# Seven block products for half of the gated-conv tiles, masked exponents and chunks from both ends in the SSD of a hybrid encoder

## Chip, cores, metric

The kernel runs on one core of one Trainium2 chip. The metric is device time in microseconds (us) of one execution; three runs are taken and their median counts. TensorE (PE) multiplies, VectorE (DVE), ScalarE (ACT) and GpSimd (POOL) work elementwise, SyncE (SP) issues the DMA transfers. Each engine takes its instructions in the order in which the built program lists them and waits on semaphores for the others.

## What is computed

A batch of one sequence of 1,024 tokens with 1,024 features goes through two layers, all in fp32. The change lies in the first, which multiplies the input by one weight matrix, feeds two head groups, and multiplies their outputs by a second matrix:

```python
z, xbc, dt_raw, sc_bg, sc_cg, sc_h, sc_gate = _split(x @ w_in, EVEN_SIZES)
xs, bm, cm = _split(silu(depthwise_conv(xbc, conv_w, (2, 1)) + conv_b), (SSD_INNER, 512, 512))
# A: SSD in both directions, chunks of 128 tokens, 4 groups of 4 heads, dt = softplus(dt_raw + bias)
cs = cumsum(dt * a)                               # within a chunk
L  = exp(where(l >= s, cs[l] - cs[s], -inf))      # decay inside a chunk, per head
y_diag = einsum(C B^T * L, x * dt)
state  = state * exp(cs[-1]) + einsum(B, exp(cs[-1] - cs), x * dt)
y_off  = einsum(C, state, exp(cs))
y_a = rms_norm((y_fwd + y_bwd) * silu(z), norm_g)
# B: short gated convolution
y_b = sc_bg * depthwise_conv(sc_cg * sc_h, sc_conv_w, (1, 1)) * silu(sc_gate)
out = layer_norm(alpha * x + concat(y_a, y_b) @ w_out)
```

## The kernel before

Every fp32 product is made of three fp32r products: an operand is cast to fp32r (`hi`, on ScalarE) and the rest is subtracted (`lo`, on VectorE, `split`), and hi·hi, hi·lo and lo·hi are summed in PSUM. A weight tile is 1,024 x 128; applied to all tokens it takes eight steps (`op_fm`, one per 128 input rows), each of six matmuls of 512 columns (`mm6`): 48 matmuls, shown as `gps`. The first layer has 48 such tiles: 16 for x, B and C of the SSD (each followed by a convolution of four taps on VectorE, `cacc`, and a SiLU, `xfm`), and 32 for the gated convolution, called `br` (four projections for each of eight blocks of 128 channels; the tile results are `bru`, `bra`, `brt`). z is computed token block by token block (`zps`).

`main_plan` writes the order of the work by hand. The SSD runs over four head groups. A group has a second phase (`op_p2`, `op_p2s`; the first is the projection) in which each of the eight chunks is transposed (`xps`) and its state is computed (`sps`) and added to the forward scan; `op_p2b` then runs the backward scan, six serial steps of a decay on GpSimd and an addition on VectorE (`hin`). In the third phase `op_p3f` builds a chunk's decay matrix times C·B^T: two broadcasts from DRAM (`E`, `tb`), Relu in eight pieces of 128 columns, `Dm` in four, a maximum, an Exp of 512 columns, two products, and the split into `Mh`, `Ml`. `op_p3x` splits the state and x. `op_p3b` multiplies: `yo` from the state, `yd` from `Mh` and `Ml`, one block of eight `yd` matmuls a chunk; the sums `to` and `ta` follow on VectorE and GpSimd.

Between these, `pull(n)` takes n steps of projection tiles from a queue: 6 ahead of the second phase (`FB`), 4 ahead of the third (`FC`), 7 after each chunk of the third (`F3`). They fill TensorE while the other engines prepare the next chunk. x of the next group goes to the front of the queue at the third phase, B and C behind it. The tile framework's scheduler then may move instructions of one engine ahead of others that wait.

Weight tiles come by DMA into two rotating buffers (`wraw`) and are split one tile ahead. At the start x arrives in eight pieces through four buffers of its own (`xraw`), is split, and feeds the small product for dt (`dtg`). At the end, the normalised SSD output is read back, scaled, transposed (`yat`) and split beside the last `br` tiles (`op_ya`, half a row block at a time), and `outproj0` multiplies (`ops`).

## Time and profile before

| | us |
|---|---|
| median of three runs (1444.60 to 1447.18) | 1445.21 |
| the profiled execution | 1445.73 |
| its span, first to last instruction | 1444.0 |
| TensorE busy | 1416.2 |
| VectorE busy | 921.9 |
| ScalarE busy | 749.1 |
| GpSimd busy | 480.5 |

The profile was taken in one execution. Busy times of TensorE overlap between neighbouring matmuls, so its rate is read from how many start in a stretch. The SSD lies between about 65 us (first `zps`) and 705 us (last `yd`); the tail of the gated tiles ends at 728 us and the output product of the first layer follows.

### The profile page before, as it was taken

The page shows a single profiled execution, that of the slowest core. Times are in us where ns is not written, and L with a number is a line of the kernel's source. Part 1 is how long each engine was busy: PE and PEld are TensorE (multiplying, and loading weights), DVE is VectorE, ACT ScalarE, POOL GpSimd, SP SyncE. Part 2 cuts the span into 40 slices and gives each one's busy share as a digit, 9 for nine tenths or more (in the row PEclk, how much of TensorE's full clock was granted, in tenths as well). Part 3 has the DMA queues.
Part 4 walks back from the last instruction along what each step waited for, and adds up shares of the span by engine and source line. Part 5 has one row for each costly group of instructions (what it writes and reads, how often), then busy time and mean ns, then how long its engine had stood idle before and what let it go on. Part 6 is the DMA issues. An engine that isn't in the chain of part 4 may idle for free.

```text
span 1444.0 us, 20351 instructions
## 1 busy us (share of the span) xinstructions
PE 1416.2 (98%) x7454; PEld 1208.9 (84%) x7454; DVE 921.9 (64%) x1608; ACT 749.1 (52%) x1567; POOL 480.5 (33%) x479
## 2 busy tenths in 40 slices
PE   7999999999999999999989999999999999999997
PEld 5898888888898888988868888898888888988886
DVE  5837666666687665647683543733326888888485
ACT  5447654576447773566443332522224788888510
...
DMA packets 46483, 118.57 MB, mean 82 GB/s; under 512 B 5808, under 2 KB 10288, under 8 KB 46384
## 3 DMA queue, kind: packets, MB, share of 16 engines
...
## 4 chain that ended last, share of the span: by engine, by line
PE 44%; DVE 4%; issue 1%; ACT 1%; DMA 0%; POOL 0%; DVEq 0%; ACTq 0%; POOLq 0%
PE ops L377 4%; PE ops L378 4%; PE ops L380 4%; PE tps L1211 3%; PE fps L371 3%; PE fps L372 3%; PE fps L370 3%; PE o1ps L377 2%; PE o1ps L380 2%; PE o1ps L378 2%; PE yps L1226 2%; PE sps L370 2%; PE sps L372 2%; PE sps L371 2%; PE yps L1225 2%
## 5 line engine op out<-in xcount | busy, mean ns | idle before, releaser
L377 PE MATMUL gps<-xhi,whi 128*128 128x512 f32 x768 | 302.2, 394 | 0.0
L378 PE MATMUL gps<-xlo,whi 128*128 128x512 f32 x768 | 301.7, 393 | 0.0
L380 PE MATMUL gps<-xhi,wlo 128*128 128x512 f32 x768 | 242.6, 393 | 0.0
L249 DVE TENSOR_TENSOR wlo<-wraw,whi 128x1024 fp32r<-128x1024 f32 x100 | 137.5, 1377 | 109.4 <-ACT whi L248 99.5
L248 ACT CAST whi<-wraw 128x1024 fp32r<-128x1024 f32 x100 | 104.7, 1049 | 131.4 <-DMA wraw<-in_wt_dram 41.3
L377 PEld LDWEIGHTS gps<-xhi,whi 128*128 128x128 f32 x768 | 144.4, 188 | 29.0
L378 PEld LDWEIGHTS gps<-xlo,whi 128*128 128x128 f32 x768 | 144.4, 188 | 29.0
L380 PEld LDWEIGHTS gps<-xhi,wlo 128*128 128x128 f32 x768 | 142.9, 188 | 28.7
L1197 POOL TENSOR_SCALAR pt<-pt,sm 128x1024 f32<-128x1024 f32 x64 | 72.9, 1140 | 114.2 <-DVE sm L1196 63.3
L467 POOL TENSOR_TENSOR xdl<-xd,xdh 128x512 fp32r<-128x512 f32 (+1 forms) x32 | 36.9, 1153 | 206.5 <-ACT xdh L466 166.0
L467 DVE TENSOR_TENSOR PT<-tps,PT 128x512 fp32r<-128x512 f32 x128 | 84.1, 681 | 12.6 <-ACT PT L466 12.4
L1191 DVE TENSOR_REDUCE nm<-sps 128x1 f32<-128x1024 f32 x64 | 77.9, 1217 | 9.5 <-PE sps L372 9.2
L467 POOL TENSOR_TENSOR hl<-hin,hh 128x512 fp32r<-128x512 f32 (+1 forms) x32 | 38.7, 1210 | 135.4 <-ACT hh L466 135.4
L814 POOL TENSOR_TENSOR rs<-rs,neghalf 128x1 f32<-128x1 f32 x16 | 12.9, 808 | 209.4 <-DMA wraw<-in_wt_dram 81.4
L1195 ACT ACTIVATE pt<-sps,nm 128x1024 f32<-128x1024 f32 x64 | 71.8, 1122 | 17.4 <-DVE nm L1192 13.1
L466 ACT CAST PT<-tps 128x512 fp32r<-128x512 f32 x128 | 69.9, 588 | 16.2 <-PE tps L1211 15.6
L370 PE MATMUL fps<-x1hi,whi 128*128 128x512 f32 x192 | 74.9, 390 | 0.0
L372 PE MATMUL fps<-x1hi,wlo 128*128 128x512 f32 x192 | 74.8, 389 | 0.0
L371 PE MATMUL fps<-x1lo,whi 128*128 128x512 f32 x192 | 74.7, 389 | 0.0
L370 PE MATMUL zps<-whi,xhi 128*128 128x256 f32 x256 | 73.9, 289 | 0.0
L372 PE MATMUL zps<-whi,xlo 128*128 128x256 f32 x256 | 72.4, 283 | 0.0
L371 PE MATMUL zps<-wlo,xhi 128*128 128x256 f32 x256 | 72.3, 282 | 0.0
...
## 6 DMA issues: line engine op xcount, KB each, us to landing
wraw<-in_wt_dram SPq DMA_DIRECT2D x100, 512.0 KB, 3.6
...
```

The source lines that it names most:

```text
L248: nc.scalar.copy(out=hi, in_=raw)
L249: nc.vector.tensor_tensor(out=lo, in0=raw, in1=hi.bitcast(F32), op=ALU.subtract)
L370: nc.tensor.matmul(out, shi, mhi, start=start, stop=False)
L371: nc.tensor.matmul(out, shi, mlo, start=False, stop=False)
L372: nc.tensor.matmul(out, slo, mhi, start=False, stop=stop)
L377: nc.tensor.matmul(out, shi, mhi, start=start, stop=False)
L378: nc.tensor.matmul(out, shi, mlo, start=False, stop=False)
L380: nc.tensor.matmul(out, slo, mhi, start=False, stop=stop)
L467: lo_eng.tensor_tensor(out=lo, in0=src, in1=hi.bitcast(F32), op=ALU.subtract)
L1191: V.tensor_reduce(out=nm, in_=ps, axis=AX.X, op=ALU.max)
L1195: A.activation(out=pt, in_=ps, func=AF.Exp, bias=nm, scale=ATT_SCALE, accum_out=sm)
L1197: GP.tensor_scalar(out=pt, in0=pt, scalar1=sm, scalar2=1.0, op0=ALU.mult, op1=ALU.mult)
```

## The change

Sixteen of the 32 `br` tiles (channel blocks 4 to 7) leave the SSD. They form eight pairs, two projections of the same channels each, and run behind the SSD. A pair is a 2 x 2 block product (two tiles by two halves of the input rows, against two halves of the input rows by two halves of the tokens), computed with seven block products in place of eight (`op_sp`, `PRODS`), each of 4 x 3 matmuls of 512 columns. The sums of weight blocks are made for the next pair meanwhile (`op_sw`), the sums of x blocks once, into four tiles (`op_tp`). Three PSUM banks a pair, A, B and D, collect the products; a bank that goes on collecting is copied first (`snap`) and subtracted parts are added afterwards (`comb`).

In the SSD, `op_p3f` now loads both directions in one broadcast, adds a mask of 0 or -1e30 in one VectorE instruction of 1,024 columns, and takes eight Exp with ln(dt) - cs as the bias, so that the decay, the triangle and dt come in one step. Chunks are taken from both ends in the second phase (0, 7, 1, 6, ...) and from the middle in the third (3, 4, 5, 2, ...); what a scan can't yet add is added in `op_p2b`, in both directions by turns. `F3` is 6, `FB` 4, and there is no pull ahead of the third phase. B and C of the next group go to the front of the queue together with x. The x pieces at the start use the weight buffers, of which there are three; x tiles hold hi and lo together; `op_ya` takes a whole row block.

```diff
-F2, F3, FB, FT, FC = 0, 7, 6, 4, 4
+F2, F3, FB, FC = 0, 6, 4, 0
+J0 = 4
+C2 = (0, 7, 1, 6, 2, 5, 3, 4)
+C3 = (3, 4, 5, 2, 6, 1, 7, 0)
...
-    for j in range(8):
...
+    for j in range(J0):
...
+        while any(s[1][0] in ("B", "C", "X") for s in queue):
+            pull(1)
     ops.append(("end",))
-    for c in range(NB):
-        pull(FT)
+    ops.append(("tp", 2))
+    pull(4)
+    ops.append(("tp", 3))
+    pull(4)
+    ops += [("sw", 0, i) for i in range(SW_N)]
+    pull(len(queue))
+    ops.append(("sw", 1, 0))
+    for n in range(NP):
+        for i in range(7):
+            ops.append(("sp", n, i))
...
+SW_N = 6
+YA_P = (1, 2)
+PAIRS = [p for j in range(J0, 8) for p in ((("br", 1, j), ("br", 2, j)), (("br", 3, j), ("br", 0, j)))]
+NP = len(PAIRS)
...
+    V.tensor_scalar(out=dt, in0=dt, scalar1=1e-37, scalar2=None, op0=ALU.max)
+    nc.scalar.activation(out=dt, in_=dt, func=AF.Ln)
+    V.tensor_tensor(out=k.eb, in0=dt, in1=k.cs, op=ALU.subtract)
...
-        raw = dtp.tile([P, 2, HALF], F32, name="xraw", tag="xraw", bufs=4)
+        raw = view(W.pool.tile([P, 1024], F32, name="xraw", tag="wraw", bufs=RAWB), 2)
...
+        for d in range(2):
+            n, o = c + 1 - 2 * d, 256 * d
+            if not 0 <= n < NB:
+                continue
+            src, dst = sps[:, o:o + 256], hin[:, n, o:o + 256]
+            if 0 <= c - 1 + 2 * d < NB and (c - 1 + 2 * d) in st["seen", d]:
+                V.tensor_tensor(out=dst, in0=src, in1=h_decay(g, c, d), op=ALU.add)
+                st["seen", d].add(c)
+            elif c == (0, NB - 1)[d]:
+                A.copy(out=dst, in_=src)
+                st["seen", d].add(c)
+            else:
+                A.copy(out=dst, in_=src)
+                st["late", d].append(c)
+
...
-        E, tb = t2("E"), t2("tb")
+        E2 = tp.tile([P, 2, 512], F32, name="E2", tag="E2", bufs=E2B)
+        E, tb = E2[:, 0], E2[:, 1]
         hs = slice(512 * g, 512 * g + 512)
-        nc.sync.dma_start(out=E, in_=k.crow[c, 0:1, hs].partition_broadcast(P))
-        nc.sync.dma_start(out=tb, in_=k.crow[c, 1:2, hs].partition_broadcast(P))
-        Dm = t2("Dm")
+        nc.sync.dma_start(out=E2, in_=k.crow[c:c + 1, :, hs].partition_broadcast(P))
+        E4 = E2.rearrange("p d (h l) -> p d h l", h=HPG)
+        V.tensor_tensor(out=E4, in0=E4, in1=bc_mid(k.mask, 2, HPG), op=ALU.add)
         for h in range(HPG):
-            hh = 4 * g + h
-            sl = slice(P * h, P * h + P)
-            for d, t in ((0, E), (1, tb)):
-                A.activation(out=t[:, sl], in_=t[:, sl], func=AF.Relu, scale=-1.0, bias=cs4[:, c, d, hh:hh + 1])
-            A.activation(out=Dm[:, sl], in_=k.sgn, func=AF.Identity, scale=k.dtd[:, c, hh:hh + 1], bias=k.dtb[:, c, hh:hh + 1])
-        V.tensor_tensor(out=E, in0=E, in1=tb, op=ALU.max)
-        A.activation(out=E, in_=E, func=AF.Exp, scale=-1.0)
-        V.tensor_tensor(out=E, in0=E, in1=Dm, op=ALU.mult)
+            for d in range(2):
+                A.activation(out=E4[:, d, h], in_=E4[:, d, h], func=AF.Exp, bias=eb4[:, c, d, 4 * g + h:4 * g + h + 1])
+        V.tensor_tensor(out=E, in0=E, in1=tb, op=ALU.add)
         cb = tb[:, P:256]
         A.copy(out=cb, in_=cbp[:, P:256])
         V.tensor_tensor(out=cb, in0=cbp[:, 0:P], in1=cb, op=ALU.add)
-        V.tensor_tensor(out=cb, in0=cb, in1=k.onei, op=ALU.mult)
         V.tensor_tensor(out=view(E, HPG), in0=view(E, HPG), in1=bc_mid(cb, 1, HPG), op=ALU.mult)
...
+    def op_tp(kk):
+        ra, rb = (W.pool.tile([P, 1024], F32, name="xtraw", tag="wraw", bufs=RAWB) for _ in range(2))
+        for r, q in ((ra, kk), (rb, kk + 4)):
+            nc.sync.dma_start(out=view(r, 2), in_=a["xT"][:, :, q, :].rearrange("h p t -> p h t"))
+        a0, a1, b0, b1 = ra[:, 0:HALF], ra[:, HALF:S], rb[:, 0:HALF], rb[:, HALF:S]
+        for o, p, q in ((a0, a1, a0), (a1, b1, a1), (b1, b1, a0), (b0, b0, b1)):
+            V.tensor_tensor(out=o, in0=p, in1=q, op=ALU.subtract)
+        t = big(k, "xT4").rearrange("p (s a t) -> p s a t", s=2, a=4)
+        for i, r in ((0, ra), (2, rb)):
+            split(nc, t[:, 0, i:i + 2, :], t[:, 1, i:i + 2, :], view(r, 2), V)
+        T[kk] = t
+
...
+        r1, r2 = st["r"]
+        h1, h2 = halves(r1), halves(r2)
...
+        if i == 1:
+            st["L11"], st["L12"] = wsplit(W.pool, (("whi", 3), ("wlo", 3)), r1)
+        elif i == 2:
+            t = k.w2.tile([P, HALF], F32, name="s3t", tag="s3t", bufs=1)
+            GP.tensor_tensor(out=t, in0=h1[0], in1=h2[0], op=ALU.subtract)
+            s3 = k.w2.tile([P, 2, HALF], F32R, name="s3", tag="s3", bufs=2)
+            split(nc, s3[:, 0], s3[:, 1], t, V)
+            st["S3"] = (s3[:, 0], s3[:, 1])
+        elif i == 3:
+            GP.tensor_tensor(out=h2[0], in0=h2[0], in1=h2[1], op=ALU.add)
+            st["S1"], st["L22"] = wsplit(W.pool, (("whi", 3), ("wlo", 3)), r2)
+        elif i == 4:
+            V.tensor_tensor(out=h1[0], in0=h2[0], in1=h1[0], op=ALU.subtract)
+            V.tensor_tensor(out=h1[1], in0=h1[1], in1=h1[0], op=ALU.subtract)
+        else:
+            st["S2"], st["S4"] = wsplit(k.w2, (("b4h", 2), ("b4l", 2)), r1)
...
+    PRODS = (("L11", 0, "A"), ("L12", 1, "B"), ("S2", "T2", "A"), ("S3", "T3", "D"), ("S1", "T1", "A"), ("L22", "T4", "D"), ("S4", 3, "A"))
+    TI = {"T1": 0, "T3": 1, "T4": 2, "T2": 3}
+
+    def op_sp(n, i):
+        st = sp[n]
+        left, right, bank = PRODS[i]
+        if bank not in st:
+            st[bank] = k.pb.tile([P, 512], F32, name="s" + bank, tag="pb")
+            fresh = True
+        else:
+            fresh = False
+        ps = st[bank]
+        wh, wl = (view(t, 4) for t in st.pop(left))
+        for kk in range(4):
+            if right in TI:
+                mh, ml = T[kk][:, 0, TI[right], :], T[kk][:, 1, TI[right], :]
+            else:
+                mh, ml = xhl(right // 2, 4 * (right % 2) + kk)
+            for m, (s_, x_) in enumerate(((wh, mh), (wh, ml), (wl, mh))):
+                PE.matmul(ps, s_[:, kk, :], x_, start=fresh and kk == 0 and m == 0, stop=kk == 3 and m == 2, skip_group_check=True)
...
+        if i == 0:
+            st["p1"] = snap(ps)
+            if first:
+                br["u"] = t4("bru")
+        elif i == 1:
+            c = br["u"][:, lo] if first else cv("c11")
+            comb(c, ps, st.pop("p1"))
+            if not first:
+                silu2(0, c)
+        elif i == 2:
+            st["v"] = snap(ps)
+        elif i == 3:
+            st["d7"] = snap(ps)
+        elif i == 4:
+            if first:
+                comb(br["u"][:, hi], ps, st.pop("d7"))
+            else:
+                c = cv("c22")
+                comb(c, ps, st.pop("d7"))
+                GP.tensor_tensor(out=br["a"][1], in0=c, in1=br["a"][1], op=ALU.mult)
...
```

Three places in the built programs, before and after.

VectorE, one chunk of the third phase in head group 1 (the second of four), before: from a chunk's `to` to the next `Ml`.

```order
L748 TENSOR_TENSOR to<-yo,ecs 128x512
L599 TENSOR_TENSOR bra<-gps,bra 128x512 x2
L759 TENSOR_TENSOR ta<-yd,ta 128x256
L249 TENSOR_TENSOR wlo<-wraw,whi 128x1024
L760 TENSOR_TENSOR ta<-yd,ta 128x256
L712 TENSOR_TENSOR E<-E,tb 128x512
L714 TENSOR_TENSOR E<-E,Dm 128x512
L717 TENSOR_TENSOR tb<-cbp,tb 128x128
L718 TENSOR_TENSOR tb<-tb,consts 128x128
L719 TENSOR_TENSOR E<-E,tb 128x512
L467 TENSOR_TENSOR Ml<-E,Mh 128x512
```

The same engine and group after; numbers behind E tell two chunks' tiles apart, and `E<-E,consts` is the mask addition.

```order
L763 TENSOR_TENSOR E_2454<-E_2454 128x512
L759 TENSOR_TENSOR E_2568<-E_2568,consts 128x1024
L275 TENSOR_TENSOR wlo<-wraw,whi 128x1024
L807 TENSOR_TENSOR ta<-yd,ta 128x256
L585 SCALAR_TENSOR_TENSOR xfm<-cth,cacc 128x512
L580 SCALAR_TENSOR_TENSOR cacc<-gps,vec,cacc 128x511
L766 TENSOR_TENSOR E_2454<-cbp,E_2454 128x128
L808 TENSOR_TENSOR ta<-yd,ta 128x256
L580 SCALAR_TENSOR_TENSOR cacc<-gps,vec,cacc 128x510
L767 TENSOR_TENSOR E_2454<-E_2454 128x512
L763 TENSOR_TENSOR E_2568<-E_2568 128x512
L580 SCALAR_TENSOR_TENSOR cacc<-gps,vec,cacc 128x512
```

Two E instructions and one of 128 columns went, the wide mask addition came, and steps of two chunks and of an x tile's convolution now stand interleaved.

VectorE, ahead of the second phase of head group 1 (it begins with the first `bhl`), before:

```order
L547 SCALAR_TENSOR_TENSOR cacc<-gps,vec,cacc 128x511
L552 SCALAR_TENSOR_TENSOR xfm<-cth,cacc 128x512
L249 TENSOR_TENSOR wlo<-wraw,whi 128x1024
L467 TENSOR_TENSOR bc<-xfm,bc 128x512
L547 SCALAR_TENSOR_TENSOR cacc<-gps,vec,cacc 128x511
L467 TENSOR_TENSOR bhl<-xps,bhl 128x128
```

And after:

```order
L759 TENSOR_TENSOR E_2357<-E_2357,consts 128x1024
L763 TENSOR_TENSOR E_2328<-E_2328 128x512
L636 TENSOR_TENSOR bra<-gps,bra 128x512 x2
L275 TENSOR_TENSOR wlo<-wraw,whi 128x1024
L808 TENSOR_TENSOR ta<-yd,ta 128x256
L763 TENSOR_TENSOR E_2357<-E_2357 128x512
L807 TENSOR_TENSOR ta<-yd,ta 128x256
L808 TENSOR_TENSOR ta<-yd,ta 128x256
L496 TENSOR_TENSOR bhl<-xps,bhl 128x128
```

Mask and sum of the group's first two chunks (`E_2328`, `E_2357`) moved ahead of its second phase; the convolution of C that stood there now comes earlier, inside the third phase.

SyncE's DMA queue at the start, before, from the constants on (two x pieces stand ahead of this):

```order
L277 DMA consts<-in_consts_dram 128x640
L498 DMA xraw<-in_xT_dram 128x2x512 x2
L236 DMA wraw<-in_wt_dram 128x1024 x2
L498 DMA xraw<-in_xT_dram 128x2x512
L398 DMA alog<-in_alog_dram 128x32
```

And after:

```order
L308 DMA consts<-in_consts_dram 128x640
L531 DMA xraw<-in_xT_dram 128x2x512
L429 DMA alog<-in_alog_dram 128x32
L431 DMA dsk<-in_dsk_dram 128x32
L343 DMA posi<-in_pos_dram 128x8
L531 DMA xraw<-in_xT_dram 128x2x512
L345 DMA invf<-in_invf_dram 128x16
L531 DMA xraw<-in_xT_dram 128x2x512 x2
L262 DMA wraw<-in_wt_dram 128x1024
```

The first weight tile moved from behind four x pieces to behind six.

## Rows read from the trace of the kernel before

**Rows 1.** The page, busy time of each engine: us, share, instructions.
```profile
PE 1416.2 (98%) x7454; PEld 1208.9 (84%) x7454; DVE 921.9 (64%) x1608; ACT 749.1 (52%) x1567; POOL 480.5 (33%) x479
```

**Rows 2.** Windows: from:to, length, then each engine's busy us and instructions, clock, DMA.
```profile
139.10:213.40 74.30, 74.30 (x355) 61.96 (x354) 52.60 (x80) 49.77 (x128) 35.06 (x38) 1.00 0.34 96
302.20:379.10 76.90, 76.90 (x367) 64.17 (x366) 49.73 (x77) 50.95 (x129) 36.77 (x39) 1.00 0.30 93
469.60:541.20 71.60, 71.60 (x344) 59.78 (x343) 48.46 (x76) 50.37 (x129) 37.03 (x40) 1.00 0.35 100
972.00:1008.00 36.00, 36.00 (x161) 29.80 (x160) 14.63 (x27) 9.33 (x12) 7.64 (x7) 1.00 0.17 50
```

**Rows 3.** VectorE by line and shape, 30 to 760 us: busy us, mean ns | idle before.
```profile
L249 DVE TENSOR_TENSOR wlo<-wraw,whi 128x1024 fp32r<-128x1024 f32 x58 | 77.2, 1333 | 37.5 <-ACT whi L248 27.6 <-PE dps L407 7.0 <-DMA yad<-yg 2.4
L547 DVE SCALAR_TENSOR_TENSOR cacc<-gps,vec,cacc 128x512 f32<-128x512 f32 x48 | 35.9, 748 | 0.6
L719 DVE TENSOR_TENSOR E<-E,tb 128x512 f32<-128x512 f32 x32 | 26.7, 833 | 0.9
...
L467 DVE TENSOR_TENSOR Ml<-E,Mh 128x512 fp32r<-128x512 f32 x32 | 25.2, 788 | 14.9 <-ACT Mh L466 14.8
...
L552 DVE SCALAR_TENSOR_TENSOR xfm<-cth,cacc 128x512 f32<-128x512 f32 x24 | 16.8, 702 | 11.7 <-ACT cth L549 11.5
L748 DVE TENSOR_TENSOR to<-yo,ecs 128x512 f32<-128x512 f32 x24 | 16.4, 683 | 0.0
...
L759 DVE TENSOR_TENSOR ta<-yd,ta 128x256 f32<-128x256 f32 x32 | 13.5, 423 | 60.8 <-POOL ta L757 59.9 <-PE gps L380 0.9
...
L585 DVE TENSOR_TENSOR bru<-gps,bru 128x1024 f32<-128x1024 f32 x8 | 9.8, 1221 | 5.4 <-PE gps L380 5.4
...
L717 DVE TENSOR_TENSOR tb<-cbp,tb 128x128 f32<-128x128 f32 x32 | 9.0, 281 | 0.0
```

**Rows 4.** Timeline of VectorE in head group 1: start us, us, instruction, idle before.
```profile
281.72 0.89 DVE L467 TENSOR_TENSOR Ml<-E,Mh 128x512 fp32r<-128x512 f32 x1 [0.35 <-ACT Mh L466]
...
297.07 0.68 DVE L714 TENSOR_TENSOR E<-E,Dm 128x512 f32<-128x512 f32 x1
297.67 0.28 DVE L717 TENSOR_TENSOR tb<-cbp,tb 128x128 f32<-128x128 f32 x1
...
301.51 0.68 DVE L467 TENSOR_TENSOR Ml<-E,Mh 128x512 fp32r<-128x512 f32 x1
```

**Rows 5.** Timeline of TensorE, the first two chunks of the third phase there.
```profile
294.62 0.23 PE L752 MATMUL yd<-xs,Mh 128*128 128x128 f32 x1
...
295.43 0.36 PE L699 MATMUL cbp<-bc 128*128 128x256 f32 x1
...
295.69 0.45 PE L377 MATMUL gps<-xhi,whi 128*128 128x512 f32 x1
...
306.64 0.40 PE L370 MATMUL yo<-hh,bc 128*128 128x512 f32 x1
306.88 0.40 PE L371 MATMUL yo<-hl,bc 128*128 128x512 f32 x1
...
308.04 0.22 PE L752 MATMUL yd<-xs,Mh 128*128 128x128 f32 x1
```

**Rows 6.** Timeline of TensorE where the output product begins.
```profile
734.49 0.50 PE L378 MATMUL ops<-wlo,ahi 128*128 128x512 f32 x1 [1.00 <-DVE wlo L249]
...
741.10 0.66 PE L784 MATMUL yat<-consts,yab 128*128 128x128 f32 x4 [3.55 <-DVE yas L786]
...
742.38 0.63 PE L377 MATMUL ops<-whi,ahi 128*128 128x512 f32 x1
742.80 0.63 PE L378 MATMUL ops<-wlo,ahi 128*128 128x512 f32 x1
```

**Rows 7.** Timeline of ScalarE at the start.
```profile
12.17 1.14 ACT L466 CAST xhi<-xraw 128x512 fp32r<-128x512 f32 x2 [0.21 <-DMA xraw<-in_xT_dram]
13.45 1.05 ACT L248 CAST whi<-wraw 128x1024 fp32r<-128x1024 f32 x1
```

**Rows 8.** Timeline of TensorE at the start.
```profile
15.39 0.39 PE L377 MATMUL gps<-xhi,whi 128*128 128x512 f32 x1
```

**Rows 9.** ScalarE by line and shape, 30 to 760 us, columns as in rows 3.
```profile
L711 ACT ACTIVATE Dm<-consts,dtb,dtd 128x128 f32<-128x128 f32 x128 | 52.8, 484 | 0.0
...
L713 ACT ACTIVATE E<-E 128x512 f32<-128x512 f32 x32 | 20.0, 626 | 10.0 <-DVE E L712 9.9
...
L363 ACT ACT_TABLE_LOAD x1 | 1.3, 1283 | 0.0
```

More of the change, by code (lines that the diff above doesn't have):

```diff
@@ L100, in main_plan @@
         pull(FB)
-        for c in range(NB):
+        for i, c in enumerate(C2):
             ops.append(("p2", g, c))
@@ L252, in split, with release @@
             self.load(i + 2)
+    def release(self):
+        self.limit = len(self.seq)
+        self.split(self.used + 1 + self.ahead)
     def get(self, key):
@@ L271, in setup @@
     cs = k.const.tile([P, 640], F32, name="consts")
-    k.ident, k.up, k.lo, k.sgn, k.onei = (cs[:, 128 * i:128 * i + 128] for i in range(5))
+    k.ident, k.up, k.lo = (cs[:, 128 * i:128 * i + 128] for i in range(3))
+    k.mask = view(cs[:, 384:640], 2)
     k.vec = k.const.tile([P, V_N], F32, name="vec")
@@ L555, in layer0_main, with br_conv @@
     br = {}
+    def br_conv(u, j):
+        hs = [slice(0, HALF), slice(HALF, S)]
+        w = lambda i: k.vec[:, V_SCW + 3 * j + i:V_SCW + 3 * j + i + 1]
+        br["a"] = []
+        for h in range(2):
+            acc = cvp.tile([P, 512], F32, name="bra", tag="bra", bufs=2)
+            A.mul(out=acc, in_=u[:, hs[h]], mul=w(1))
+            for i, sh in ((0, -1), (2, 1)):
+                a0 = 1 if h == 0 and sh < 0 else 0
+                a1 = HALF - 1 if h == 1 and sh > 0 else HALF
+                lo = HALF * h + sh
+                V.scalar_tensor_tensor(out=acc[:, a0:a1], in0=u[:, lo + a0:lo + a1], scalar=w(i), in1=acc[:, a0:a1], op0=ALU.mult, op1=ALU.add)
+            br["a"].append(acc)
     def fm_finish(key, ps):
@@ L574, in fm_finish @@
                 sl = slice(HALF * h, HALF * h + HALF)
-                v = conv_half(ps, 8 + 4 * q + g, st["xfm"][:, 2, sl] if q == 0 else None, h)
+                v = conv_half(ps, 8 + 4 * q + g, st["xfm"][:, 2 + q, sl], h)
                 split(nc, st["bc"][:, 2 * q, sl], st["bc"][:, 2 * q + 1, sl], v, V)
@@ L585, in fm_finish @@
                 V.tensor_tensor(out=u, in0=ps, in1=u, op=ALU.mult)
[L586 to L596 removed]
+                br_conv(u, j)
             elif q == 0:
@@ L615, in op_fm @@
         wh, wl = view(whi, KD), view(wlo, KD)
-        mm6(nc, halves(ps), wh[:, kk, :], wl[:, kk, :], [t[:, kk, :] for t in xhi], [t[:, kk, :] for t in xlo], kk == 0, kk == KD - 1)
+        mm6(nc, halves(ps), wh[:, kk, :], wl[:, kk, :], *zip(*(xhl(h, kk) for h in range(2))), kk == 0, kk == KD - 1)
         if kk == KD - 1:
@@ new lines, in layer0_main, with op_sw, wsplit @@
+    sp = [dict() for _ in PAIRS]
+    def op_sw(n, i):
+        st = sp[n]
+        if i == 0:
+            st["r"] = []
+            for key in PAIRS[n]:
+                r = W.pool.tile([P, 1024], F32, name="sraw", tag="wraw", bufs=RAWB)
+                nc.sync.dma_start(out=r, in_=a["wt"][W.idx[key]])
+                st["r"].append(r)
+            return
+        r1, r2 = st["r"]
+        h1, h2 = halves(r1), halves(r2)
+        def wsplit(pool, tags, r):
+            hi, lo = (pool.tile([P, 1024], F32R, name=t, tag=t, bufs=b) for t, b in tags)
+            split(nc, hi, lo, r, V)
+            return list(zip(halves(hi), halves(lo)))
+        if i == 1:
[14 more added lines that the diff above has]
+            st["S2"], st["S4"] = wsplit(k.w2, (("b4h", 2), ("b4l", 2)), r1)
@@ new lines, in snap, with comb, silu2, gate @@
+    def snap(ps):
+        t = k.w2.tile([P, HALF], F32, name="snap", tag="snap", bufs=3)
+        A.copy(out=t, in_=ps)
+        return t
+    def comb(out, ps, t):
+        V.tensor_tensor(out=out, in0=ps, in1=t, op=ALU.add)
+    def silu2(h, src):
+        th = cv("brt")
+        A.activation(out=th, in_=src, func=AF.Tanh, scale=0.5)
+        V.scalar_tensor_tensor(out=th, in0=th, scalar=1.0, in1=src, op0=ALU.add, op1=ALU.mult)
+        br["th", h] = th
+    def gate(h, j):
+        acc = br["a"][h]
+        GP.tensor_tensor(out=acc, in0=acc, in1=br.pop(("th", h)), op=ALU.mult)
+        nc.sync.dma_start(out=k.ybd[j, :, HALF * h:HALF * h + HALF], in_=acc)
@@ new lines, in layer0_main @@
+    k.ay = {}
+    def op_ya(c):
+        if c // 2 not in k.ay:
+            k.ay[c // 2] = big(k, f"ay{c // 2}").rearrange("p (s a t) -> p s a t", s=2, a=KD)
+        o = (c % 2) * P
+        t = k.ay[c // 2]
+        y = W.pool.tile([P, S], F32, name="yab", tag="wraw", bufs=RAWB)
+        nc.sync.dma_start(out=y, in_=k.yad[c])
+        A.mul(out=y, in_=y, mul=k.rinv[:, c:c + 1])
+        ps = k.pa.tile([P, 1024], F32, name="yat", tag="pa")
+        for f in range(KD):
+            PE.transpose(out=ps[:, P * f:P * f + P], in_=y[:, P * f:P * f + P], identity=k.ident)
+        V.tensor_tensor(out=view(y, KD), in0=view(ps, KD), in1=bc_last(k.vec[:, V_NG:V_NG + KD], P), op=ALU.mult)
+        split(nc, t[:, 0, :, o:o + P], t[:, 1, :, o:o + P], view(y, KD), V)
```

182 lines of the change are left out of this document (95 added, 87 removed).

## Prediction

> **What bounds the kernel now.** I read the page first. TensorE is busy for 98% of the span [rows 1], but its matmuls overlap and this share cannot show a lost microsecond, so I went to rates. In a stretch of the second layer that holds matmuls of 512 columns alone, 161 start in 36 us at a granted clock of 1.00 [rows 2]: one every 0.225 us, at the upper of the two clock levels, 2.4 GHz. Then I read the timeline of TensorE. Inside the SSD a matmul that fills (gps) and one that belongs to a chunk (yo, yd) follow each other with nothing between [rows 5], and the windows over the third phase of three head groups show TensorE busy for all of 74.3, 76.9 and 71.6 us [rows 2]. So TensorE's own work sets the time from 30 us to about 730 us, and every matmul that is taken out there is worth its 0.225 us, as long as nobody else becomes late.
>
> Next I asked who is the next latest in the third phase. VectorE is busy 49.7 of 76.9 us and ScalarE 51.0 [rows 2]. What matters is the lead: VectorE's last step for a chunk (Ml) against the first matmul that reads it (yd). In head group 1 the first chunk's Ml ends at 281.72 + 0.89 = 282.6 and its yd starts at 294.6, 12.0 us later; the second's ends at 302.2 and its yd starts at 308.0, 5.9 us later [rows 4, 5]. This lead is bought with filling matmuls, and the change halves the stock of them.
>
> **The change part by part.** All sums are made against the profiled execution, 1445.73 us with a span of 1444.0; the median of the three runs, 1445.21, lies 0.5 below it, and that is taken off at the end. A difference under 0.2%, 2.9 us, can't be told from none.
>
> *Seven products.* Two tiles take 2 x 48 = 96 matmuls of 512 columns; as seven block products they take 7 x 4 x 3 = 84. Eight pairs save 96 matmuls: 96 x 0.225 = **-21.6 us** [rows 2]. Other TensorE work keeps its counts.
>
> *The third phase with less to fill.* 128 filling steps of the 16 moved tiles leave the SSD (the pull after a chunk falls from 7 steps to 6, ahead of the second phase from 6 to 4, ahead of the third from 4 to 0), while B and C of the next group, the tiles that cost VectorE most, move from behind the third phase into it. I counted what stands in the changed program between the second and the eighth Ml of a group on VectorE, and between the second and the eighth block of yd on TensorE. Head group 1 has on TensorE 157 gps, 18 yo, six blocks of yd and five cbp: 157 x 0.225 + 18 x 0.235 + 6 x 0.81 + 5 x 0.26 = 45.7 us [rows 2, 5]. VectorE has 83 instructions: 13 on E at 0.833, 19 cacc at 0.748, 7 xfm at 0.702, 6 mask additions, 6 cb at 0.281, 6 Ml at 0.788, 4 wlo at 1.333, 15 of 256 columns at 0.423 and 7 of 512 columns from PSUM at 0.683 [rows 3]. The mask addition (1,024 columns, both inputs in SBUF) is not in the trace. From below it is the 1.221 of 1,024 columns read from PSUM (bru), from above two E rows, 1.67; I take 1.333, the row of wlo, which has the same width and both inputs in SBUF [rows 3]. That makes 60.8 us. It must not be compared with TensorE as it stands: a VectorE instruction of 0.68 us at 297.07 is followed by the next at 297.67 [rows 4], so back to back each overlaps the last by 0.08, and 83 x 0.08 = 6.6 come off: 54.2 us. The same count gives 56.4 against 46.2 in group 0, 57.6 against 45.7 in group 2, and 41.1 against 51.1 in group 3, which has gated tiles alone to fill with. So VectorE, which had 49.7 us of work in 76.9, now has 8.5 to 11.9 us more than TensorE in three of four groups. What saves it is the lead at the second chunk. The changed program puts mask, exponents and sum of the first two chunks ahead of the group's second phase, so I take 9 us, midway between the 5.9 and the 12.0 above. With VectorE never idle the three groups stall 1.2, 0 and 2.9 us, 4.1 in all; with 5% idle (ScalarE's casts lie between its steps) 4.2, 2.4 and 5.9, 12.5 in all. I take **+9**, 3 a group; the ends are 0 and 32 (below).
>
> The port is where a rule speaks against the change. The E row, both inputs in SBUF, takes 0.833; the to row, one input from PSUM, 0.683 at the same width [rows 3]; GpSimd is busy 36.8 of 76.9 us [rows 2]. The Trainium skill ("SBUF — State Buffer", Who interferes with whom) says that a VectorE instruction with two SBUF inputs contends with GpSimd's reads, and that the loser waits for the whole instruction. The 0.15 us between the rows agrees. By the rule that extra would grow with GpSimd's share, 48% to some 65% when the same 37 us lie in 57: 0.05 us more on about 30 such instructions, 1.5 us a group, and the sum would end 4.5 us later.
>
> *Decays by masked exponents.* Of a chunk, ScalarE loses four Dm at 0.484 and one Exp of 512 columns at 0.626, 2.6 us, and keeps eight pieces of 128 columns [rows 9]. It was not what TensorE waited for, so this is worth nothing by itself; it shortens the way to Ml. The two broadcasts of a chunk become one of 512 KB; hidden as now by two buffers of lead. Four more table loads at 1.283 [rows 9] are 5 us of ScalarE, two of them in a second phase where it is half idle: nothing.
>
> *Chunks from both ends.* The backward scan of six serial steps becomes chains of three and two, and the first chunk in the third phase no longer needs the scan's last result. TensorE does not wait there now, so nothing is gained; it pays for the 4 filling steps that went.
>
> *The start.* The x tiles now share the three weight buffers. Before, the first weight tile is cast at 13.45 and the first gps starts at 15.39, while half of x is still to come [rows 7, 8]. In the changed queue the first weight stands behind six x tiles instead of four, and dtg has 24 matmuls ahead of the first gps instead of 16. Two x tiles more on the queue are about 2 x 1.4 us (13.45 less 12.17, from cast to cast [rows 7]), a buffer's wait on top, less 8 dtg at 0.225: **+2**, from 0 to 5.
>
> *The pairs.* 84 x 0.225 = 18.9 us of TensorE each. VectorE has per pair three splits of a tile (4.0), half a tile's split and two subtractions (2.1), three sums (2.1), and the gate or the convolution (1.4 or 4): about 10 to 12 us by [rows 3], so it is covered. A bank is read out while one other product, 12 x 0.225 = 2.7 us, runs, and a 1,024-column instruction in front of the reader can use that up: **+1.5** over eight pairs, from 0 to 17 (0.3 us at each of 56 products).
>
> *The hand-over* to the output product now loses 3.55 us of waiting, some 8 matmuls at 0.43 instead of 0.225 after it, the lower clock level [rows 6], and a microsecond more: about 6. The changed program has the same kind of end, six row blocks to normalise and transpose in 20 us of TensorE work, and, ahead of the pairs, four transformed x tiles (about 5 us of VectorE each) beside 27 us of matmuls. **0**, from -6 to +5.
>
> Sum: -21.6 + 9 + 2 + 1.5 + 0 = -9.1; 1445.7 - 9.1 - 0.5 = **1436 us**.
>
> **Rivals.** (1) *VectorE keeps up.* If the lead at the second chunk is 12 us, the deficits of 8.5 to 11.9 are all covered and the third phase costs nothing: -21.6 + 3.5 = -18.1, **1427**. For it: TensorE is never late behind VectorE today, at 65% load; against it: the sums above leave no margin. (2) *The third phase becomes VectorE's.* With the lead of today's second chunk, 5.9, and VectorE idle a tenth of its time, the stalls are 56.4/0.9 - 46.2 - 5.9 = 10.6, and 8.6 and 12.4 likewise, 31.6 together: -21.6 + 31.6 + 3.5 = +13.5, **1459**, slower. It decides from 6 us of stall a group on. For it: ScalarE keeps 51.0 less six chunks' 2.6, some 35 us, in the same shorter stretch, and each of the two waits for the other in order. (3) *The gain is just given back*, 5 to 7 us a group: -21.6 + 18 + 3.5, **1445**. (4) *The pairs wait for banks*, 0.3 us at each of 56 products: +17 in place of 1.5, **1452**. That fewer matmuls run is certain by count; that the change does not do what it says is no rival.
>
> **How the numbers follow.** Forecast 45%, with its own range 1430 to 1443; rival 1 17%; rival 2 20%; rival 3 12%; rival 4 6%. Faster is rival 1 and all but 2 of the forecast's 45: 60%. Same is rival 3, those 2 and half of rival 4: 17%. Slower is rival 2 and the other half of rival 4: 23%. The range goes from 1424 (rival 1 with half of the hand-over's loss returned) to 1453 (rival 4, and the milder part of rival 2).
>
> **What would show it.** Right: TensorE waits on Ml in the third phase of head groups 0 to 2, in the later chunks, some 3 us a group, and not in group 3; a pair takes about 19 us; VectorE over 90% busy in those stretches. Wrong: no wait on Ml (rival 1); waits of over 6 us a group, or the lower clock level inside the SSD (rival 2); sA, sB or sD waiting on snap or on the sums (rival 4); a first gps later than 20 us.

## The result and the profile after

The changed kernel takes **1498.99 us** (median of 4 runs, 1494.91 to 1500.58), the kernel before 1445.87 in the same comparison: **1.0363 times as long, 95% interval 1.0338 to 1.0388**. The forecast was 1436, range 1424 to 1453. The profiled execution has a span of 1495.7 us.

Busy time of each engine, from the page after (before: [rows 1]):
```profile
PE 1425.4 (95%) x7358; PEld 1209.0 (81%) x7358; DVE 1001.4 (67%) x1615; ACT 726.0 (49%) x1452; POOL 557.4 (37%) x507
```
The 96 matmuls are gone, VectorE has 80 us more, GpSimd 77. The output product starts at 779.5 us where it started at 728.6; from there on both kernels take equally long. So I went to the third phases, one window for each head group (from:to, length, busy us and instructions of PE, PEld, DVE, ACT, POOL, then clock):
```profile
117.60:204.40 86.80, 78.73 (x370) 65.36 (x369) 77.96 (x110) 53.47 (x132) 53.16 (x50) 0.94 0.33 97
247.10:334.90 87.80, 77.58 (x355) 63.59 (x354) 79.48 (x112) 50.98 (x129) 54.09 (x53) 0.92 0.37 102
383.70:473.10 89.40, 80.99 (x367) 66.21 (x366) 78.89 (x113) 51.60 (x130) 53.59 (x50) 0.92 0.32 98
511.40:600.40 89.00, 82.83 (x375) 67.94 (x373) 73.80 (x96) 44.99 (x112) 61.67 (x55) 0.92 0.40 113
```
VectorE is busy for 83 to 91% of them, 65 to 71% in [rows 2]; TensorE, never idle there before, is idle for 6 to 10 us, and its granted clock fell from 1.00 to 0.92 to 0.94. Set against the median start-to-start time of each kind of matmul, the four groups, second phases included, lose about 12.0, 13.3, 10.2 and 6.9 us to idle time and 5.0, 6.3, 6.4 and 6.2 us to matmuls at the lower clock level: **42 and 24 us, 66 in all**; before it was 0.1. Around them little is lost: the start about 2 us more than before, the stretch of the pairs 4.

How the two losses hang together, in the timeline of TensorE (start, us, instruction, idle before):
```profile
277.30 0.40 PE L403 MATMUL yo<-hh,bc 128*128 128x512 f32 x1
279.98 0.33 PE L800 MATMUL yd<-xs,Mh 128*128 128x128 f32 x1 [2.28 <-POOL xs L496]
...
284.33 0.80 PE L408 MATMUL gps<-x,whi 128*128 128x512 f32 x1 [3.02 <-DVE cacc L580]
284.93 0.63 PE L409 MATMUL gps<-x,whi 128*128 128x512 f32 x1
285.36 0.63 PE L408 MATMUL gps<-x,whi 128*128 128x512 f32 x1
```
After the two waits the matmuls start 0.43 us apart in place of 0.225, 1.2 GHz in place of 2.4. TensorE seldom waits for Ml itself; it waits for banks that the convolutions read out, and for GpSimd's parts of xs and hl (waits from 100 to 600 us: total, times, longest):
```profile
PE gps L408 <- DVE cacc L580: 11.3, 6, 3.0
PE yo L402 <- POOL hl L496: 8.8, 5, 2.9
PE yd L800 <- POOL xs L496: 7.5, 5, 2.3
PE yo L401 <- ACT hh L495: 2.5, 2, 2.3
```
VectorE's lines by shape, 207 to 600 us (busy, mean ns; before: [rows 3]):
```profile
L275 DVE TENSOR_TENSOR wlo<-wraw,whi 128x1024 fp32r<-128x1024 f32 x25 | 36.9, 1477 | 3.3 <-ACT whi L274 3.0 <-PE zps L402 0.2
L759 DVE TENSOR_TENSOR E<-E,consts 128x1024 f32<-128x1024 f32 x23 | 30.4, 1322 | 16.7 <-DMA E<-crow 16.7
L763 DVE TENSOR_TENSOR E<-E 128x512 f32<-128x512 f32 x24 | 22.4, 934 | 4.1 <-ACT E L762 4.1
L767 DVE TENSOR_TENSOR E<-E 128x512 f32<-128x512 f32 x24 | 21.0, 874 | 0.2
L496 DVE TENSOR_TENSOR Ml<-E,Mh 128x512 fp32r<-128x512 f32 x24 | 20.6, 858 | 3.0 <-ACT Mh L495 3.0
L580 DVE SCALAR_TENSOR_TENSOR cacc<-gps,vec,cacc 128x512 f32<-128x512 f32 x24 | 17.8, 742 | 0.1
L585 DVE SCALAR_TENSOR_TENSOR xfm<-cth,cacc 128x512 f32<-128x512 f32 x16 | 14.0, 876 | 0.0
L796 DVE TENSOR_TENSOR to<-yo,ecs 128x512 f32<-128x512 f32 x18 | 12.3, 681 | 0.0
```
The mask addition costs 1.32, close to the 1.333 I took. Rows that read PSUM keep their time (cacc 0.742, to 0.681); rows with both inputs in SBUF grew (xfm 0.70 to 0.88, Ml 0.79 to 0.86, wlo 1.33 to 1.48, and the product with C·B^T, L719 before and L767 now, 0.83 to 0.87). And VectorE now waits for a transfer, in the timeline of head group 1:
```profile
275.90 1.55 DVE L496 TENSOR_TENSOR Ml<-E,Mh 128x512 fp32r<-128x512 f32 x1
...
280.10 1.07 DVE L767 TENSOR_TENSOR E<-E 128x512 f32<-128x512 f32 x1
282.40 1.22 DVE L759 TENSOR_TENSOR E<-E,consts 128x1024 f32<-128x1024 f32 x1 [1.23 <-DMA E<-crow]
```
Its fetch is issued when Ml has freed the buffer, and lands 4.9 us later (queue of SP):
```profile
277.48 0.37 SPq L757 DMA_DIRECT2D E<-crow  x1
```

### The profile page after: what moved, and what is told of

It reads as the page before. It is cut to its first block, busy times and chain, and to the rows that moved or that the text cites. A ratio compares the mean times of both kernels' runs of the same rounds, so it can differ in the third digit from the quotient of the medians.

```text
span 1495.7 us, 20072 instructions
## 1 busy us (share of the span) xinstructions
PE 1425.4 (95%) x7358; PEld 1209.0 (81%) x7358; DVE 1001.4 (67%) x1615; ACT 726.0 (49%) x1452; POOL 557.4 (37%) x507
## 4 chain that ended last, share of the span: by engine, by line
PE 51%; DVE 3%; DMA 2%; ACT 2%; issue 1%; POOL 0%; DVEq 0%; SPq 0%; POOLq 0%; ACTq 0%
PE sA L912 5%; PE ops L409 3%; PE ops L408 3%; PE ops L411 3%; PE tps L1396 3%; PE fps L403 3%; PE fps L402 3%; PE fps L401 3%; PE sD L912 2%; PE o1ps L408 2%; PE o1ps L411 2%; PE o1ps L409 2%; PE yps L1411 2%; PE sps L401 2%; PE sps L403 2%; PE sps L402 2%
## 5 line engine op out<-in xcount | busy, mean ns | idle before, releaser
L408 PE MATMUL gps<-x,whi 128*128 128x512 f32 x512 | 210.5, 411 | 11.4 <-DVE cacc L580 11.3
L409 PE MATMUL gps<-x,whi 128*128 128x512 f32 x512 | 208.0, 406 | 0.0
L275 DVE TENSOR_TENSOR wlo<-wraw,whi 128x1024 fp32r<-128x1024 f32 x84 | 119.6, 1424 | 89.2 <-ACT whi L274 84.8
L411 PE MATMUL gps<-x,wlo 128*128 128x512 f32 x512 | 167.9, 405 | 3.0 <-DVE wlo L275 2.9
L274 ACT CAST whi<-wraw 128x1024 fp32r<-128x1024 f32 x84 | 88.1, 1049 | 128.9 <-PE ops L411 61.0
L408 PEld LDWEIGHTS gps<-x,whi 128*128 128x128 f32 x512 | 100.6, 196 | 34.0 <-DVE cacc L580 9.0
L411 PEld LDWEIGHTS gps<-x,wlo 128*128 128x128 f32 x512 | 98.8, 195 | 25.1 <-DVE wlo L275 4.3
L409 PEld LDWEIGHTS gps<-x,whi 128*128 128x128 f32 x512 | 100.9, 197 | 20.5
L762 ACT ACTIVATE E<-E,eb 128x128 f32<-128x128 f32 x256 | 78.8, 389 | 58.9 <-DVE E L759 58.2
L993 POOL TENSOR_TENSOR rs<-rs,neghalf 128x1 f32<-128x1 f32 x16 | 12.9, 810 | 213.9 <-DVE nm L1028 146.1
L401 PE MATMUL zps<-whi,x 128*128 128x256 f32 x256 | 74.4, 291 | 3.0 <-DVE to L796 1.6
L402 PE MATMUL zps<-wlo,x 128*128 128x256 f32 x256 | 73.0, 285 | 0.0
L403 PE MATMUL zps<-whi,x 128*128 128x256 f32 x256 | 72.9, 285 | 0.0
```

The source lines that it names most:

```text
L274: nc.scalar.copy(out=hi, in_=raw)
L275: nc.vector.tensor_tensor(out=lo, in0=raw, in1=hi.bitcast(F32), op=ALU.subtract)
L401: nc.tensor.matmul(out, shi, mhi, start=start, stop=False)
L402: nc.tensor.matmul(out, shi, mlo, start=False, stop=False)
L403: nc.tensor.matmul(out, slo, mhi, start=False, stop=stop)
L408: nc.tensor.matmul(out, shi, mhi, start=start, stop=False)
```

## Experiments

Each time is a median, with its ratio to the kernel before on the same chip. Between 1499 and 1445 lie 54 us. The changed kernel also has 21.6 us less TensorE work, so about 75 us are lost in all, and a version without pairs has to be set against these 75.

**The third phase as changed.**

*Three buffers* (E2B 3, T2B 9). 

> The changed kernel with three buffers instead of two for the exponents that a chunk fetches (E2); one temporary of 512 columns fewer pays for it. In the trace of the changed kernel the fetch of a chunk is issued when Ml of the chunk two before has read its buffer (VectorE's mask addition starts at 282.40, when the fetch issued at 277.48 lands), and VectorE waits 16.7 us for such fetches in head groups 1 to 3. Theory A (VectorE has more work in the third phase than TensorE has left, and that sets the time): the waits go and little comes of it, since VectorE is 88% busy there as it is: 1480 to 1499. Theory B (the loop fetch, mask, exponents, Ml, fetch through two buffers sets the pace of the chunks): the 4.9 us landing leaves the loop in 24 or more chunks, 1468 or less, with the granted clock back near 1.00 in the third phases.


1501.68, 1.0392 [1.0376, 1.0409]: no gain; A's range is missed by 2.7 on the same side. But VectorE's waits for the fetch hardly went (18.5 us between 100 and 600 us, 22.1 in the changed kernel), so the run shows only that a third buffer does not help as the order stands. The waits themselves go in "The change, held" below.

*No mask addition.*
```diff
-V.tensor_tensor(out=E4, in0=E4, in1=bc_mid(k.mask, 2, HPG), op=ALU.add)
-A.activation(..., func=AF.Exp, bias=eb4[...])
+A.activation(..., func=AF.Exp)
```


> The changed kernel without the mask addition and without the bias of the exponents: 32 VectorE instructions of 1.32 us are left out, and the decays are not the right ones. Theory A (VectorE's load): 32 x 1.32 = 42 us of VectorE go out of stretches that VectorE bounds, some of it gives way to its own waits: 25 to 45 faster than the changed kernel, 1454 to 1474. Theory B (the loop through two buffers): the addition is one step of a loop that spans two chunks, so half of it comes back: some 20, 1475 to 1484. A third theory, that ScalarE or GpSimd sets the pace: within 8 of 1499.


1475.20, 1.0206 [1.0188, 1.0224]: 24 us for 42 us of VectorE, between A's range and B's. Without the addition ScalarE reads the fetch first again, so VectorE's 22 us of waiting for it go too (29.5 us of waiting for ScalarE's Exp come); the run does not tell the two apart.

*B and C behind* (`to_front` of B, C after the chunks; F3 5, FB 0). 

> The changed kernel with B and C of the next head group behind the third phase again, as in the kernel before; 5 filling steps a chunk in place of 6 and none ahead of the second phase, so that the same stock of gated tiles is used and 16 gated tiles stay as 8 pairs. Theory A: per group the four half tiles of B and C (six cacc at 0.74, two xfm and two bc at 0.7 to 0.9 for each tile, 14 us) leave VectorE's share of the third phase and lie behind it, beside 21.6 us of TensorE work; TensorE gives up 8 steps (10.8 us) there too, so the phase gets shorter but the shortage remains in part: 1450 to 1475. Theory B (loop through two buffers): a chunk still takes 8 to 9 us in the third phase, and 3 x 21.6 us of TensorE work now lie outside it: 1510 or more.


1487.54, 1.0299 [1.0277, 1.0321]: 11 us, outside both ranges. With 48 to 58 us of VectorE in six chunks of 60 to 66, TensorE still stalled, now for ScalarE's hh (12.8 us), and VectorE waited 32 us for the fetch in place of 22. VectorE's share of busy time was not all of it.

*Less GpSimd work.*
```diff
-split(nc, hh_[:, cols], hl_[:, cols], hin[:, c, cols], nc.gpsimd)
+A.copy(out=hh_[:, cols], ...); A.copy(out=hl_[:, cols], ...)
```
and likewise for xs and the product with dsum. 

> The changed kernel with three of GpSimd's six instructions of a chunk's third phase replaced by plain copies on ScalarE (both halves of hl and xs, and the product with dsum; the splits' lower parts are not subtracted, so the result differs): GpSimd loses 1.47 + 1.05 + 0.97 of some 6.5 us a chunk, ScalarE gains about 1.4. Theory A: VectorE's own load hardly changes; what comes back is that its rows with both inputs in SBUF (xfm 0.88, E 0.93 and 0.87, wlo 1.48) return part of the way to those of the kernel before (0.69, 0.83, 1.37), 2 to 4 us a group: 1480 to 1495. Theory C (the two engines delay each other, and that is the larger part of the loss): the rows return to the old values, TensorE's waits on hl and xs (16.3 us) go, 1470 or less.


1480.99, 1.0249 [1.0233, 1.0265]: 18 us, in A's range. VectorE's lines of this run, same stretch:
```profile
L275 DVE TENSOR_TENSOR wlo<-wraw,whi 128x1024 fp32r<-128x1024 f32 x25 | 33.5, 1342 | 4.3 <-ACT whi L274 4.2
L759 DVE TENSOR_TENSOR E<-E,consts 128x1024 f32<-128x1024 f32 x23 | 28.6, 1245 | 27.7 <-DMA E<-crow 27.7
...
L763 DVE TENSOR_TENSOR E<-E 128x512 f32<-128x512 f32 x23 | 17.4, 757 | 4.0 <-ACT E L762 4.0
L496 DVE TENSOR_TENSOR Ml<-E,Mh 128x512 fp32r<-128x512 f32 x24 | 17.4, 724 | 1.4 <-ACT Mh L495 1.4
L585 DVE SCALAR_TENSOR_TENSOR xfm<-cth,cacc 128x512 f32<-128x512 f32 x16 | 14.0, 875 | 0.2 <-ACT cth L582 0.2
```
With GpSimd's work nearly halved, E and Ml are shorter by 0.13 to 0.18 and wlo by 0.14; xfm is not. Part of the 18 us may also be that TensorE no longer waits for GpSimd's hl and xs; the run changes both. What VectorE won there it partly waited away at the fetch (16.7 to 27.7 us).

*More TensorE work.*
```diff
+if extra and kk < KD - 1:
+    PE.matmul(ps[:, HALF:S], wl[:, kk, :], xhl(1, kk)[0], start=False, stop=False)
```


> The changed kernel with one more matmul in seven of eight filling steps of the third phase (the small correction product of one half is added a second time): 168 matmuls, 37.8 us of TensorE work at the upper clock level. Theory A: TensorE has idle time there, and the lower clock level after it costs 24 us; work that fills the idle time costs nearly nothing and brings the clock back: 1485 to 1508, granted clock in the third phases 0.95 or more. If TensorE were the bound there: 1533 to 1540.


1527.15, 1.0570 [1.0546, 1.0593]: a miss. 28 of the 37.8 us came on top, and the granted clock in the third phases rose only a little, to 0.93 in group 0 and 0.95 to 0.96 in the others. Six chunks took 67 to 74 us in place of 58 to 68, with nearly the same idle time (39 us for 42): idle time is not spare time, since it lies at particular waits.

**Filling and decays apart.**

*All 32 tiles inside* (J0 8, F3 7, FB 6, FC 4, B and C behind, no pairs). 

> The changed kernel without pairs: all 32 gated tiles are plain tiles again, with the filling of the kernel before (7 steps a chunk, 6 ahead of the second phase, 4 ahead of the third, B and C behind the third phase); the masked exponents, the chunks from both ends and the x tiles in the weight buffers stay. Theory A (the third phase needs about 10 us a chunk for VectorE, ScalarE and GpSimd together, 60 to 65.6 us for six chunks without B and C, and TensorE must have that much to do): 7 x 1.35 + 1.8 = 11.3 us of TensorE work a chunk are enough, 1440 to 1450. Theory D (the masked exponents or the order of the chunks cost the time by themselves): the loss stays, 1465 or more.


1494.30, 1.0341 [1.0314, 1.0367]. Theory A falls as the only cause: with full filling 49 us are still lost. With the matmuls counted equal, that is 49 of 75; full filling, without pairs, gave about a third back.

*Before, with less cover.* 

> The kernel before, with its own decays and chunk order, but with the filling of the changed one: 6 steps a chunk, 4 ahead of the second phase, none ahead of the third, B and C of the next head group in the third phase; the 16 gated tiles stand behind the SSD as plain tiles, so the number of matmuls is that of the kernel before. Theory A: the loss of the changed kernel's SSD (some 66 us) comes without any other part of the change, and a little more, since the old decays give VectorE 0.6 us a chunk more: 1500 to 1535. Theory D: little, 1465 or less.


1491.62, 1.0320 [1.0305, 1.0335]. D falls as the only cause too, and A's range is missed by 8. The test is less clean than planned: 44 of the 52 us lost in the SSD lie in groups 1 and 2 (6 come back behind it), more than half of them ahead of the group's first yd, in few long waits (9.7 and 6.3 us among them). There C's convolved tile lies in the convolution's own buffers, which the change had moved elsewhere; that this makes the waits is not shown. Group 3, with six steps of gated tiles a chunk, lost nothing.

*All inside, old decays* (the decay code and constants of before). 

> The version with all 32 tiles inside and full filling (1494), now with the decays of the kernel before. What is left of the change is the chunk order, the x tiles in the weight buffers and the end of the SSD. Theory E: 1442 to 1455. Theory F: 1475 or more.


1457.16, 1.0076 [1.0059, 1.0093], 37 us below the new decays. Its third phases lose 0.3 us in all; 9 of the 11 us to the kernel before lie where the output product begins. So with full filling the chunk order costs TensorE nothing in the chunks, and F falls. Windows over the third phase of group 1, old decays and then new:
```profile
273.50:377.20 103.70, 103.70 (x500) 86.85 (x498) 74.67 (x116) 70.61 (x178) 54.27 (x57) 1.00 0.36 106
```
```profile
284.30:393.30 109.00, 101.16 (x462) 83.57 (x461) 75.39 (x105) 51.51 (x134) 56.40 (x57) 0.94 0.36 99
```
The new decays free ScalarE (51.5 for 70.6 us), which TensorE did not wait for, and VectorE, hardly busier but standing at the fetch, delays TensorE.

*The change with old decays.* 

> The changed kernel with the decays of the kernel before (Relu pieces, Dm, max, Exp, two separate fetches into temporaries of 512 columns, ln(dt) out of the bias); pairs, filling, place of B and C and chunk order stay as changed. The version with all tiles inside lost 49 us with full filling, a chunk taking 12.5 us there, and each of its mask additions starts 4.9 to 6.7 us after a fetch that was issued as Ml of the chunk two before ended. Theory E (the masked exponents make VectorE the first reader of the fetch and tie it to two buffers; that loop, with VectorE's queue in order, is the cause): most of the 54 us come back though VectorE gets 0.6 us a chunk more, 1435 to 1465. Theory A (VectorE's load against the filling that is left): 1499 or more. Theory F (the chunk order with its late scan): 1490 or more.


1519.91, 1.0512 [1.0487, 1.0537]: E fails here. Where filling is short the old decays are 21 us worse. The built order runs ahead of the plan: between first and last yd it has 304, 300 and 265 filling matmuls in groups 0 to 2 and 106 in group 3 (the changed kernel 192 to 210 in each), and group 3 alone loses 37 us, the wait for the first pair 7 more.

Four of these runs cross filling and decays. With the matmuls counted equal, the changed kernel loses 75 us, with full filling in place of its own 49, with the old decays in place of its own 96, and with both 11, of which 0.3 in the third phases. So each of the two edits is enough for a loss, and the loss goes only when both are undone. (Full filling here also means no pairs; "Four pairs, old decays" below has both pairs and full filling.)

**The fetch.**

*All inside, three buffers.* 

> The version with all 32 tiles inside and full filling (1494), now with three buffers for the fetched exponents and one temporary of 512 columns fewer. Theory E, if the loop through two buffers is what binds with full filling: the loop spans three chunks, 25 us / 3 = 8.4 a chunk, below TensorE's 11.3: 1445 to 1462. If what counts is that VectorE's queue stands still for any fetch: 1475 or more. Theory F: 1485 or more.


1496.65, 1.0353 [1.0337, 1.0368]: not the number of buffers. The built order puts a chunk's mask addition right behind the Ml that frees its buffer, with two and with three, and VectorE waits 73.5 us for fetches just issued.

*No fetch* (the mask addition reads the mask twice). 

> The version with all 32 tiles inside and full filling (1494), with the fetch of the exponents left out: the mask addition reads the mask twice and the exponents have no bias, so the decays are not the right ones; every instruction of VectorE and ScalarE stays. Theory G (VectorE's queue stands still at each mask addition until a fetch of 5 us has landed, 67 us in all, and everything behind it is late): 1448 to 1464. If the new instructions' own time is what counts: 1480 or more.


1469.55, 1.0171 [1.0155, 1.0186].

*Three buffers, mask addition held.*
`k.mls` lists the Ml in order; what the block issues is put behind the named one on the same engine.
```diff
+with k.tc.issue_after(k.mls[-2]) if len(k.mls) > 1 else ExitStack():
     V.tensor_tensor(out=E4, in0=E4, in1=bc_mid(k.mask, 2, HPG), op=ALU.add)
```


> The version with all 32 tiles inside and three buffers (1497), where in addition the order is told to put a chunk's mask addition behind Ml of the chunk two before; its fetch is issued after Ml of the chunk three before, a chunk of some 11 us earlier. Nothing else is changed. Theory G: VectorE's waits for the fetch go, 1446 to 1466. If the waits only move (to the exponents, or to ScalarE): 1480 or more.


1471.64, 1.0181 [1.0166, 1.0197]. VectorE's longest waits, with two buffers, and held:
```profile
DVE E L743 <- DMA E<-crow: 68.7, 26, 5.7
DVE wlo L259 <- ACT whi L258: 51.8, 17, 9.7
```
```profile
DVE wlo L259 <- ACT whi L258: 57.1, 18, 9.7
DVE zx L661 <- ACT zt L660: 40.4, 19, 3.0
```
Both runs end 6 us outside G's ranges, but agree: standing still for the fetch is 23 to 25 of the 37 us. The other 12 to 14 stay with the new decays; why is not shown. VectorE is then busy 81 of 98 us in group 1.

*The change, held.* 

> The changed kernel itself with three buffers and the same hold of the mask addition (with three buffers alone it took 1502). Theory G alone: 1440 to 1460. Theory A beside it (VectorE has 58 to 61 us of work in the 67 of six chunks, TensorE 46): VectorE's waits for the fetch, 22 us in all, go, and no more: 1472 to 1492.


1501.70, 1.0392 [1.0371, 1.0413]: nothing. Its fetch waits fell from 22 to 6 us, and GpSimd's xs and hl took their place (waits of TensorE, 100 to 600 us):
```profile
PE yd L802 <- POOL xs L496: 9.8, 9, 4.7
PE yo L402 <- POOL hl L496: 9.6, 8, 4.0
PE yo L401 <- ACT hh L495: 7.5, 5, 4.0
```
*Less GpSimd work, held.* 

> The changed kernel with less GpSimd work (1481 alone: hl, xs and the product with dsum as copies on ScalarE, results differ) and also three buffers and the mask addition held (1502 alone). If the fetch is the next limit behind the shared time of VectorE and GpSimd: VectorE waited 33 us for fetches in the run with less GpSimd work, half or more of it comes back, 1455 to 1470. If VectorE's number of instructions is all that is left: 1476 to 1486.


1472.28, 1.0173 [1.0154, 1.0192], between the two ranges: 9 us below less GpSimd work alone, 29 below the hold alone. So the fetch counts only once GpSimd's share is down: the limits stand behind each other. Six chunks of groups 0 to 2 now take VectorE 54 to 57 us, of which it works 51 to 55, so little but its own instructions is left there; that they are the last limit is argued, not tested.

**Versions meant to beat both.** None did.

*Six pairs* (J0 5, F3 6, FB 0, B and C behind). 

> A version meant to be faster than both: the changed kernel with 12 gated tiles as 6 pairs instead of 16 as 8, 6 filling steps a chunk, none ahead of the second phase, B and C behind the third phase. 6 pairs save 72 matmuls, 16.2 us; 6 x 1.35 + 1.8 = 9.9 us of TensorE work a chunk. Theory A: just short of the 10 to 10.9 us that a chunk needs, 1 to 6 us lost a group with the clock: 1435 to 1455. Theory D: 1465 or more.


1486.80, 1.0292 [1.0275, 1.0309].
*The same, old decays.* 

> A version meant to be faster than both: 12 gated tiles as 6 pairs, 6 filling steps a chunk, B and C behind the third phase (1487), now with the decays of the kernel before. 6 pairs save 16.2 us. Theory E: 1428 to 1445. Theories A and F: 1475 or more.


1494.92, 1.0337 [1.0322, 1.0353]; 28 us of it lost in group 3, where filling ran out (178 filling matmuls), and 7 in the wait for the first pair.
*Four pairs, held* (J0 6, F3 7, FB 0). 

> A version meant to be faster than both: 8 gated tiles as 4 pairs (48 matmuls, 10.8 us saved), 7 filling steps a chunk, B and C behind the third phase, three buffers and the mask addition held. Theory G, with TensorE's 11.3 us a chunk against some 9 of VectorE: 1434 to 1455. If full filling doesn't do with the new decays: 1470 or more.


1479.65, 1.0249 [1.0227, 1.0271].
*Four pairs, old decays.* 

> A version meant to be faster than both: the changed kernel with the decays of the kernel before, 8 gated tiles as 4 pairs (10.8 us of TensorE saved), 7 filling steps a chunk, B and C behind the third phase. Between the first and the last yd of a group its built order has 292 to 317 filling matmuls, the kernel before 300 to 335, the changed kernel 192 to 210. If that number decides: no stall in the third phases, some 8 us lost where the pairs begin, since no filling is left there: 1438 to 1450. If pairs or chunk order cost more: 1455 or more.


1464.74, 1.0127 [1.0112, 1.0142]. No group loses more than 1 us between its first and last yd, as the count of matmuls said, and the pairs are in; but one wait at the first pair takes more than the 10.8 us saved:
```profile
PE sA L921 <- ACT whi L499: 15.9, 1, 15.9
```

## Why the prediction was wrong

**The step that failed** is "the third phase with less to fill", put at +9 and worth 66. It let one thing alone delay TensorE: VectorE's time for six chunks, less TensorE's 46.2, 45.7 and 45.7, less a lead of 9 that is used up. Put in the time VectorE took, 67.2, 66.5 and 67.6, and the stalls come out at 12.0, 11.8 and 12.9, close to the 12.0, 13.3 and 10.2 measured. That is luck: those were lost over whole groups. For the six chunks of the sum, from the second block of yd to the eighth, TensorE took 54.9, 61.4 and 54.9 us, so it lost 8.7, 15.7 and 9.2 (the clock included), and it never ran into Ml. In head group 1 the second and the eighth chunk, VectorE and then TensorE:
```profile
261.90 0.68 DVE L496 TENSOR_TENSOR Ml<-E,Mh 128x512 fp32r<-128x512 f32 x1
...
328.42 0.68 DVE L496 TENSOR_TENSOR Ml<-E,Mh 128x512 fp32r<-128x512 f32 x1
```
```profile
272.49 0.22 PE L800 MATMUL yd<-xs,Mh 128*128 128x128 f32 x1
...
333.93 0.22 PE L800 MATMUL yd<-xs,Mh 128*128 128x128 f32 x1
```
The lead is 9.9 us at the second chunk and still 4.8 at the eighth (14.8 to 2.5 in group 0, 18.7 to 6.0 in group 2). TensorE stood at what the sum left out: the banks that cacc reads (11.3 us), GpSimd's hl and xs (16.3 us), and the clock. The held run says the same: VectorE's six chunks took 57.3, 62.5 and 59.1 us there, and no time came back. In the sum's own terms, four things were wrong.
- *VectorE's work*: 60.0, 58.6 and 60.9 us, overlaps taken off, for the forecast 56.4, 54.2 and 57.6. The count was right (84, 83 and 87 instructions; group 1 was counted at 83), the rows grew. The Trainium skill ("SBUF — State Buffer", Who interferes with whom) pointed there; by it I put 1.5 us a group, the trace has 3.3 to 4.4. The 0.15 us that I took for its sign was a weak one: xfm, with both inputs in SBUF too, took 0.702 in [rows 3].
- *VectorE's idle time*: 7 to 8 us a group for the 0 to 5% I took, 17 of 22 us in three groups at the mask addition. "Hidden as now by two buffers of lead" was wrong: before, ScalarE read the fetch first; now VectorE does, whose queue holds everything else.
- *The clock*: the lower level inside the SSD, which I named as a sign of rival 2 but gave no price, cost 24 us.
- *GpSimd*: not in the sum at all. It was busy for 60 to 69% of the third phases; with its work there nearly halved, 18 us came back.

Group 3, taken as safe, lost 13: I had left out the transformed x tiles, part of whose subtractions stands in its third phase. They do not make the loss alone: with them in place, group 3 lost nothing in the held run with less GpSimd work.

**Rival 2** came nearest, and its sign, the lower clock level inside the SSD, was seen; but it had 31.6 us of stalls for 42 and no clock, so even its 1459 was too low. **The edit that was called worth nothing** was not: with full filling the masked exponents alone cost 37 us (1494 against 1457), with the short filling of the change they gain 21 (1499 against 1520), and a rival for it was missing. **Right**: the pairs (694 matmuls in the 157.3 us from 622.2 to 779.5 at a clock of 0.99), the start, and the hand-over near 0. **The sign that I named** failed in part: TensorE waits on banks and on GpSimd, not on Ml.

Not settled: what keeps the held run with less GpSimd work 26 us above the kernel before, and so 48 above what its matmuls allow (some 38 of them lie in groups 0 to 2, 6.5 in one wait at the first pair); how much of the loss with less cover comes from B and C; and whether the chunk order costs anything when filling is short, since it was not undone alone there.
